# Gate projection in one pass with low weight columns beside the high ones, a 128-row broadcast for the mLSTM, and max scans ahead of the sums

## The chip, the cores and the metric

The program runs on one core of a Trainium2 chip. The metric is the device time of one execution in microseconds; the median of three runs of the kernel before is 877.35 us (877.31 to 877.92). An engine is named as in the profile: PE multiplies matrices (its weight loads are listed apart as PEld), DVE works on vectors, ACT applies functions and copies with a scale, POOL does small general work, and SP starts most transfers.

## The reference

One layer of an encoder over 512 tokens of width 1024. Its first third mixes tokens with two groups of heads, HGRN2 and mLSTM; cross-attention and a squared-ReLU MLP follow. The change touches the gates of the mLSTM group only:

```python
proj = xn @ w_in + b_in          # 16 of its columns are the mLSTM gates
ig_fwd, ig_bwd = ...             # input gates, 4 heads x 2 directions
lfg = log_sigmoid(m_fg)          # forget gates, 4 heads x 2 directions
# per head and direction, over time t and s <= t (or s >= t, backward):
cum   = cumsum(lfg)
log_d = cum[t] - cum[s] + ig[s]
m_t   = max(max_s log_d, cum + m)          # running maximum
d_mat = exp(log_d - m_t)
h_out = (scores * d_mat) @ v / max(|den|, exp(-m_t))
```

## The kernel before, in words

**Products in three passes.** Every large product keeps float32 accuracy by writing each operand as a high and a low part: ACT copies the high part in a rounded format and DVE subtracts it from the source (`split_out`, L222). `mm3` (L226) then issues three matmuls: high by high, high by low, low by high (L227, L228, L229).

**The weight stream.** The weights lie in 512 KB tiles in the order of use (`SEQ`). `weights` (L214) keeps three split tiles, named `wh` and `wl`, and loads a fourth ahead. A tile of the form "d" holds 128 output columns; `proj_d` (L240) makes 8 x 3 = 24 matmuls of 128x128 by 128x512 from it. Below, such a group of 24 is a column. The gate tile is one of these; only 16 of its 128 output columns are used (four each at 0, 32, 64 and 96), the others are zero.

**Chains and ticks.** Work that depends on long rows of small steps is written as generators ("chains"). `proj_d` calls `tick` (L178) after the first 12 matmuls of a column and after the column; a tick runs one chain up to its next `yield`. With several chains in the list, the number of ticks so far, odd or even, says which of the first two runs. `drain` (L191) ticks until no chain is left.

**Order on the engines.** Until L943 a planner places the instructions: on each engine it takes those that its own estimate has ready, in the order of the program, while the split of weights has precedence. So PE mostly follows the program, and small work of DVE, ACT and POOL may be placed early, or a PE step that is not ready be placed some matmuls later. From L943 the order on PE is that of the text.

**The gates.** `gates_proj` (L461) makes the gate rows (`grow`) with 24 matmuls. `gates_chain` (L471) then takes nine ticks while `hgrn_proj(0)` makes six columns: transposes of `grow` (L475) and the logarithm of the sigmoid in `lf` (L477 to L494); sums over time by triangular matmuls (L502); a transpose of `lf` from the tile `lp` into rows `lrow` (L524 to L529); four scans along 512 tokens, for each direction the running maximum `mr` and then the running sum `Fr` (L545, L547); the difference of the two, split into a high and a low half in `ar` (L550 to L552); transposes of `mr` (L556) and their exponential `em` (L558).

**The use of `ar`.** `mlstm_chain` (L594) broadcasts, for each of four heads and two directions, one row of `ar` over all 128 partitions: the column of `selr` that picks the row is the stationary operand, and two matmuls of 64 rows by 512, high and low (L601, L602), add up in PSUM. DVE adds a mask (L605), ACT takes ten exponentials of 128x128 (L612).

Of the kernel before, what the change touches and what calls it, by code (L numbers as in the profile page):

```python
# [18 lines left out]
P = 128  # L19
# [60 lines left out]
def trunk(ctx: ExitStack, tc: tile.TileContext, x, mem, wpk, vec, cst, lmask, rmask, rows, out):  # L80
# [64 lines left out]
    def small_setup():  # L145
        lmf = A4()
        nc.sync.dma_start(out=vc, in_=vec)
        nc.sync.dma_start(out=lmf[:, 0:len(LEVELS) * P], in_=lmask)
        v.tensor_copy(lm, lmf[:, 0:len(LEVELS) * P])
        le, lr = tiny(8), tiny(8)  # L150
        lg = vc[:, V_LB:V_LB + 8]
        v.tensor_tensor(out=le, in0=lg, in1=lg, op=ALU.subtract)
        sc.activation(le, le, AF.Exp)
        v.reciprocal(lr, le)
        v.tensor_tensor(out=le, in0=le, in1=lr, op=ALU.mult)
        v.tensor_tensor(out=lb[:, 0:8], in0=le, in1=le, op=ALU.subtract)
        v.tensor_scalar(out=lb[:, 8:16], in0=lb[:, 0:8], scalar1=-1.0, scalar2=1.0, op0=ALU.mult, op1=ALU.add)
        v.tensor_copy(selr, cs[:, C_SEL:C_SEL + 8])
        v.tensor_scalar(out=negb, in0=vc[:, V_FF:V_FF + 8], scalar1=-1.0, scalar2=None, op0=ALU.mult)

    selr = sb.tile([P, 8], F32R, name="selr")
# [298 lines left out]

    def gates_proj():  # L461
        gh, gl = weights(("d", "gate", 0, 0))
        ps = mmb()
        for k in range(8):
            z = slice(k * P, k * P + P)
            mm3(ps, gh[:, z], gl[:, z], xs[k][0], xs[k][1], k == 0, k == 7)
        grow = A4()
        sc.activation(grow[:, 0:512], ps, AF.Identity, bias=vc[:, V_GATE:V_GATE + 1])
        ml["grow"] = grow

    def gates_chain():  # L471
        grow = ml["grow"]
        ps = smb()
        for t in range(4):
            pe.transpose(ps[:, t * P:t * P + P], grow[:, t * P:t * P + P], ident)  # L475
        gt = sb.tile([P, 64], F32, name="gt")
        v.tensor_copy(gt[:, :].rearrange("p (w g h) -> p w g h", g=4, h=4), ap(ps, 0, [P, 4], [32, 4], [1, 4]))  # L477
        ig = ap(gt, 0, [16, 4], [1, 8])
        z = ap(gt, 8, [16, 4], [1, 8])
        w3 = lambda t: t[:, :].rearrange("p (w c) -> p w c", c=8)  # L480
        az, u, s, s2, pl = tiny(32), tiny(32), tiny(32), tiny(32), tiny(32)
        v.scalar_tensor_tensor(out=w3(az), in0=z, scalar=-1.0, in1=z, op0=ALU.mult, op1=ALU.min)
        sc.activation(u, az, AF.Exp)
        v.tensor_scalar(out=s, in0=u, scalar1=2.0, scalar2=None, op0=ALU.add)
        v.reciprocal(s, s)
        v.tensor_tensor(out=s, in0=s, in1=u, op=ALU.mult)
        v.tensor_tensor(out=s2, in0=s, in1=s, op=ALU.mult)
        v.tensor_scalar(out=pl, in0=s2, scalar1=1.0 / 17, scalar2=1.0 / 15, op0=ALU.mult, op1=ALU.add)
        for n in (13, 11, 9, 7, 5, 3, 1):
            v.tensor_tensor(out=pl, in0=pl, in1=s2, op=ALU.mult)  # L490
            v.tensor_scalar(out=pl, in0=pl, scalar1=1.0 / n, scalar2=None, op0=ALU.add)
        v.scalar_tensor_tensor(out=pl, in0=pl, scalar=-2.0, in1=s, op0=ALU.mult, op1=ALU.mult)
        lf = tiny(32)
        v.scalar_tensor_tensor(out=w3(lf), in0=z, scalar=0.0, in1=w3(pl), op0=ALU.min, op1=ALU.add)  # L494
        for _ in range(4):
            yield

        tri = A4()
        nc.sync.dma_start(out=tri[:, 0:640], in_=cst[:, NC1:NC_])
        pb = smb()  # L500
        for i, c in enumerate((C_INC, C_SUF, C_ISUF, C_PRE, C_ONE)):
            pe.matmul(pb[:, i * 32:i * 32 + 32], lhsT=tri[:, c:c + P], rhs=lf, start=True, stop=True)  # L502
        bd = sb.tile([P, 128], F32, name="bd")
        b4 = lambda g, w, dr: bd[:, g * 32 + w * 8 + dr * 4:g * 32 + w * 8 + dr * 4 + 4]
        bg = lambda g, dr: ap(bd, g * 32 + dr * 4, [8, 4], [1, 4])
        pg = lambda i, dr: ap(pb, i * 32 + dr * 4, [8, 4], [1, 4])
        igd = lambda dr: ap(gt, dr * 4, [16, 4], [1, 4])
        for dr in range(2):
            v.tensor_tensor(out=bg(0, dr), in0=igd(dr), in1=pg(2 * dr, dr), op=ALU.subtract)
            v.tensor_tensor(out=bg(1, dr), in0=igd(dr), in1=pg(2 * dr + 1, dr), op=ALU.add)  # L510
        tot = lambda w, dr: pb[:, 128 + w * 8 + dr * 4:128 + w * 8 + dr * 4 + 4]
        gp.memset(bd[:, 64:128], 0.0)
        for w in (0, 1):
            v.tensor_tensor(out=b4(2, w, 0), in0=b4(1, w, 0), in1=tot(w + 1, 0), op=ALU.add)
            v.tensor_tensor(out=b4(2, 3 - w, 1), in0=b4(1, 3 - w, 1), in1=tot(2 - w, 1), op=ALU.add)
        v.tensor_tensor(out=b4(3, 0, 0), in0=b4(2, 0, 0), in1=tot(2, 0), op=ALU.add)
        v.tensor_tensor(out=b4(3, 3, 1), in0=b4(2, 3, 1), in1=tot(1, 1), op=ALU.add)
        ml["bd"] = lambda g, w, dr, h: bd[:, g * 32 + w * 8 + dr * 4 + h:g * 32 + w * 8 + dr * 4 + h + 1]
        yield

        lp = A4()
        gp.memset(lp[:, 0:512], 0.0)
        for dr in range(2):
            v.tensor_copy(ap(lp, dr * 32, [P, 4], [1, 4]), ap(lf, dr * 4, [8, 4], [1, 4]))  # L524
        ps = smb()
        for t in range(4):
            pe.transpose(ps[:, t * P:t * P + P], lp[:, t * P:t * P + P], ident)
        lrow = grow[:, 512:1024]
        sc.activation(lrow[0:64, 0:512], ps[0:64, :], AF.Copy)  # L529
        rm = lp[:, 512:1024]  # L530
        nc.sync.dma_start(out=rm[0:64, 0:512], in_=rmask)
        yield
        fm = A4()
        Fr, mr = fm[:, 0:512], fm[:, 512:1024]
        gp.memset(Fr[0:64, 0:512], 0.0)
        gp.memset(mr[0:64, 0:512], 0.0)

        def rows_ap(t, dr):
            a = t[0:4, 0:512] if dr == 0 else t[32:36, 0:512]
            if dr == 0:  # L540
                return a
            return bass.AP(a.tensor, a.offset + 511, [list(a.ap[0]), [-1, 512]])

        for dr in range(2):
            v.tensor_tensor_scan(out=rows_ap(mr, dr), data0=rows_ap(lrow, dr), data1=rows_ap(grow, dr),  # L545
                                 initial=0.0, op0=ALU.add, op1=ALU.max)
            v.tensor_tensor_scan(out=rows_ap(Fr, dr), data0=rows_ap(rm, dr), data1=rows_ap(lrow, dr),  # L547
                                 initial=0.0, op0=ALU.mult, op1=ALU.add)
        yield
        v.tensor_tensor(out=Fr[0:64, 0:512], in0=Fr[0:64, 0:512], in1=mr[0:64, 0:512], op=ALU.subtract)  # L550
        ar = big.tile([64, 1024], F32R, name="ar")
        split_out(ar[:, 0:512], ar[:, 512:1024], Fr[0:64, 0:512])  # L552
        ml["ar"] = ar
        ps = smb()
        for t in range(4):
            pe.transpose(ps[:, t * 64:t * 64 + 64], mr[0:64, t * P:t * P + P], ident[0:64, 0:64])  # L556
        em = sb.tile([P, 32], F32, name="em")
        sc.activation(em[:, :].rearrange("p (w g h) -> p w g h", g=2, h=4), ap(ps, 0, [64, 4], [32, 2], [1, 4]), AF.Exp, scale=-1.0)  # L558
        ml["em"] = em
        yield  # L560

    mv = []
# [31 lines left out]
    def mlstm_chain(h, gate):  # L594
# [2 lines left out]
        bcol, ar, em = ml["bd"], ml["ar"], ml["em"]  # L597
        for dr in range(2):
            pa = smb()
            lw = selr[0:64, dr * 4 + h:dr * 4 + h + 1].to_broadcast([64, P])  # L600
            pe.matmul(pa, lhsT=lw, rhs=ar[:, 0:512], start=True, stop=False)  # L601
            pe.matmul(pa, lhsT=lw, rhs=ar[:, 512:1024], start=False, stop=True)  # L602
            am = T2()
            cm = cs[:, C_MF + dr * P:C_MF + dr * P + P]
            v.tensor_tensor(out=am[:, 0:512].rearrange("p (w t) -> p w t", t=P), in0=pa[:, :].rearrange("p (w t) -> p w t", t=P),  # L605
                            in1=cm.unsqueeze(1).to_broadcast([P, 4, P]), op=ALU.add)
            for ws in range(4):
                for wt in (range(ws, 4) if dr == 0 else range(0, ws + 1)):
                    gap = abs(wt - ws)
                    col = ws * 640 + ((wt - ws) * P if dr == 0 else (4 - ws) * P + wt * P)  # L610
                    src = (am if gap == 0 else pa)[:, wt * P:wt * P + P]
                    sc.activation(St[:, col:col + P], src, AF.Exp, bias=bcol(gap, ws, dr, h))  # L612
            yield
# [72 lines left out]
    gates_proj()  # L686
    chains.append(gates_chain())
    hgrn_proj(0)
    drain()
    hgrn_start(0)  # L690
    hgrn_gate(0)
    hgrn_proj(1)
# [430 lines left out]
```

## Time and profile before

| | us |
|---|---|
| median of three runs | 877.35 |
| the profiled execution | 877.47 |
| its span on the chip | 875.7 |
| DVE busy in the span | 576.2 |
| ACT busy in the span | 415.5 |
| POOL busy in the span | 67.4 |

The span runs from the first to the last instruction of the execution; 1.8 us of the profiled execution's time lie around it. A row of the timeline gives the start of an instruction in us from the start of the span, its length, its engine and line, its output and inputs with shapes, and in brackets how long the engine was idle before it and what ended that. The length of a matmul includes the time in which the next one is already running, so the cost of a matmul in a dense stream is the distance between two starts, not its length. A row of the waits gives the total, the number and the longest of the waits of one line for another.

### The profile page before, as it was taken

How to read it: one execution, taken by the hardware profiler on the slowest of the kernel's cores; microseconds unless marked ns; L12 is line 12 of the kernel's file. 1: busy time of each engine (PE TensorE's matmuls, PEld its weight loads, DVE VectorE, ACT ScalarE, POOL GpSimd, SP SyncE). 2: the span in 40 equal slices, each digit the busy share in tenths (PEclk: the TensorE clock that was granted, in tenths of full speed). 3: DMA queues.
4: the chain of work that ended last, by engine and by line, in shares of the span. 5: the costliest groups of instructions: out<-in, count | busy, mean ns of one | idle time of the engine just before them, and what ended most of it. 6: DMA issues, size and time to landing. Idle time of an engine off the chain costs nothing.

```text
span 875.7 us, 11191 instructions
## 1 busy us (share of the span) xinstructions
PE 853.6 (97%) x4198; PEld 709.3 (81%) x4198; DVE 576.2 (66%) x1006; ACT 415.5 (47%) x758; POOL 67.4 (8%) x114
## 2 busy tenths in 40 slices
PE   7999999999999999999999999999999999999995
PEld 5887888888887886888888887888888888888884
DVE  5557688779536987654655445776667656766675
ACT  5235343353358658534544355553355345435544
POOL 2000000010001000000000200002200310121001
PEclk9999999999999999999999999999999999999998
DMA  7322222311234223352212772238945993598322
GB/s 261 135 98 79 73 73 73 117 63 50 73 99 117 97 98 120 121 169 84 85 51 71 194 190 82 92 116 212 284 143 127 238 279 109 150 284 217 115 55 96
DMA packets 32680, 113.58 MB, mean 130 GB/s; under 512 B 3761, under 2 KB 3889, under 8 KB 32626
## 3 DMA queue, kind: packets, MB, share of 16 engines
q1 hardware_dynamic: 23120, 78.84, 26.1%
q0 software_dynamic: 9216, 33.56, 17.2%
q8 instruction: 33, 0.54, 0.2%
q10 hardware_dynamic: 290, 0.47, 0.1%
q14 instruction: 21, 0.17, 0.1%
HBM read 110.76 MB, written 2.10 MB: 129 GB/s over the span
## 4 chain that ended last, share of the span: by engine, by line
PE 49%; DVE 1%; ACT 0%; POOL 0%; issue 0%; POOLq 0%; ACTq 0%
PE mm L228 10%; PE mm L229 10%; PE mm L227 10%; PE sm L997 5%; PE sm L999 5%; PE sm L998 5%; PE mm L999 1%; PE mm L998 1%; PE mm L997 1%; PE sm L229 1%; PE sm L228 1%; PE sm L227 1%; PE sm L770 0%; PE sm L827 0%; DVE vv L922 0%; ACT t L756 0%
## 5 line engine op out<-in xcount | busy, mean ns | idle before, releaser
L223 ACT ACTIVATE wh<-st 128x1024 fp32r<-128x1024 f32 x133 | 140.9, 1059 | 233.1 <-PE mm L228 115.4
L224 DVE TENSOR_TENSOR wl<-st,wh 128x1024 fp32r<-128x1024 f32 x133 | 162.7, 1223 | 124.3 <-ACT wh L223 120.6
L227 PE MATMUL mm<-xT,wh 128*128 128x512 f32 x552 | 219.7, 399 | 0.0
L228 PE MATMUL mm<-xT,wh 128*128 128x512 f32 x552 | 216.4, 392 | 0.2 <-DVE xT L776 0.2
L229 PE MATMUL mm<-xT,wl 128*128 128x512 f32 x552 | 215.8, 391 | 0.0
L228 PEld LDWEIGHTS mm<-xT,wh 128*128 128x128 f32 x552 | 103.8, 188 | 22.7 <-DVE xT L776 2.0
L229 PEld LDWEIGHTS mm<-xT,wl 128*128 128x128 f32 x552 | 103.6, 188 | 21.7 <-issue 0.2
L227 PEld LDWEIGHTS mm<-xT,wh 128*128 128x128 f32 x552 | 103.8, 188 | 21.4 <-issue 1.2
L891 POOL DMA_DIRECT2D as<-in_wpk x48 | 36.6, 772 | 312.1 <-DVE wl L224 188.1
L955 DVE SCALAR_TENSOR_TENSOR t<-mm,rg 128x512 f32<-128x512 f32 x32 | 22.1, 691 | 55.2 <-PE mm L229 55.0
L229 PE MATMUL mm<-wh,yT 128*128 128x512 f32 x128 | 50.6, 395 | 0.0
L227 PE MATMUL mm<-wh,yT 128*128 128x512 f32 x128 | 50.5, 394 | 0.0
L228 PE MATMUL mm<-wl,yT 128*128 128x512 f32 x128 | 50.0, 391 | 0.0
L999 PE MATMUL sm<-wh,yT 128*128 128x512 f32 x128 | 49.8, 389 | 0.0
L998 PE MATMUL sm<-wl,yT 128*128 128x512 f32 x128 | 49.8, 389 | 0.0
L997 PE MATMUL sm<-wh,yT 128*128 128x512 f32 x128 | 49.8, 389 | 0.0
L223 ACT ACTIVATE wh<-as 128x1024 fp32r<-128x1024 f32 x24 | 25.5, 1062 | 33.3 <-PE sm L999 23.7
L224 DVE TENSOR_TENSOR wl<-as,wh 128x1024 fp32r<-128x1024 f32 x24 | 29.4, 1225 | 13.9 <-ACT wh L223 13.9
L378 PEld LDWEIGHTS sm<-a,t 128*128 128x128 f32 x224 | 30.1, 191 | 2.2 <-ACT t L368 0.4
L930 DVE TENSOR_TENSOR vv<-vv,sm 128x512 f32<-128x512 f32 x48 | 31.0, 680 | 1.2 <-PE sm L999 1.2
L368 ACT ACTIVATE t<-a 128x512 f32<-128x512 f32 x28 | 18.4, 674 | 26.3 <-DVE a L431 23.8
L378 PE MATMUL sm<-a,t 128*128 128x128 f32 x224 | 30.9, 285 | 0.0
(258 smaller groups left out, 1513.5 us busy)
## 6 DMA issues: line engine op xcount, KB each, us to landing
st<-in_wpk SPq DMA_DIRECT2D x133, 512.0 KB, 3.3
as<-in_wpk POOLq DMA_DIRECT2D x48, 512.0 KB, 6.7
gate<-in_wpk POOLq DMA_DIRECT2D x16, 512.0 KB, 7.2
as<-in_x SPq DMA_DIRECT2D x4, 512.0 KB, 6.5
vv<-in_x SPq DMA_DIRECT2D x8, 256.0 KB, 4.3
out<-vv SPq DMA_DIRECT2D x7, 256.0 KB, 2.3
a<-in_mem SPq DMA_DIRECT2D x2, 512.0 KB, 3.9
t<-in_rows SPq DMA_DIRECT2D x2, 256.0 KB, 5.9
```

The source lines that it names most:

```text
L223: sc.activation(dst_hi, src, AF.Copy)
L224: v.tensor_tensor(out=dst_lo, in0=src, in1=dst_hi.bitcast(F32), op=ALU.subtract)
L227: pe.matmul(ps, lhsT=ah, rhs=bh, start=first, stop=False)
L228: pe.matmul(ps, lhsT=ah, rhs=bl, start=False, stop=False)
L229: pe.matmul(ps, lhsT=al, rhs=bh, start=False, stop=last)
L378: pe.matmul(ps[:, z], lhsT=kc[:, z], rhs=ap(q2, w * P, [2 * L, P // (2 * L)], [512 + L, 2], [1, L]), start=True, stop=True)
L891: gp.dma_start(out=dst, in_=wpk[idx], **kw)
L930: v.tensor_tensor(out=z, in0=z, in1=ps, op=ALU.add if sign > 0 else ALU.subtract)
L955: v.scalar_tensor_tensor(out=y, in0=ps, scalar=0.0, in1=rrow[:, 0:512], op0=ALU.max, op1=ALU.mult)
L997: pe.matmul(ps, lhsT=ah, rhs=bh, start=new, stop=False, **fl)
L998: pe.matmul(ps, lhsT=ah, rhs=bl, start=False, stop=False, **fl)
L999: pe.matmul(ps, lhsT=al, rhs=bh, start=False, stop=end and k == 1, **fl)
```

## The change

It edits eight places. In `gates_proj` one DVE copy puts the 16 low columns (`gl`) into unused columns of the high tile (`gh`), 16 columns to the right of their high counterparts; two matmuls for each of eight slices remain. The low part's result comes out in rows of its own, and `gates_chain` adds it after the transpose. As the rows of `grow` no longer hold the full sum, the input gates go through the transpose of `lp` too, and a second ACT copy puts them back into rows. The two max scans come ahead of the two sum scans, with a `yield` between; the transposes of `mr` come ahead of the split of `ar`. `ar` now holds the high half in partitions 0 to 63 and the low half in 64 to 127, `selr` is written to both halves of its tile, and the broadcast is one matmul. A `drain()` goes.

```diff
-        v.tensor_copy(selr, cs[:, C_SEL:C_SEL + 8])
+        v.tensor_copy(selr[0:64, :], cs[0:64, C_SEL:C_SEL + 8])
+        v.tensor_copy(selr[64:128, :], cs[0:64, C_SEL:C_SEL + 8])
...
         gh, gl = weights(("d", "gate", 0, 0))
+
+        v.tensor_copy(ap(gh, 16, [P, 8], [32, 4], [1, 4]), ap(gl, 0, [P, 8], [32, 4], [1, 4]))
         ps = mmb()
         for k in range(8):
             z = slice(k * P, k * P + P)
-            mm3(ps, gh[:, z], gl[:, z], xs[k][0], xs[k][1], k == 0, k == 7)
+            pe.matmul(ps, lhsT=gh[:, z], rhs=xs[k][0], start=k == 0, stop=False)
+            pe.matmul(ps, lhsT=gh[:, z], rhs=xs[k][1], start=False, stop=k == 7)
...
-        v.tensor_copy(gt[:, :].rearrange("p (w g h) -> p w g h", g=4, h=4), ap(ps, 0, [P, 4], [32, 4], [1, 4]))
+        g4 = gt[:, :].rearrange("p (w g h) -> p w g h", g=4, h=4)
+        v.tensor_copy(g4, ap(ps, 0, [P, 4], [32, 4], [1, 4]))
+        v.tensor_tensor(out=g4, in0=g4, in1=ap(ps, 16, [P, 4], [32, 4], [1, 4]), op=ALU.add)
...
             v.tensor_copy(ap(lp, dr * 32, [P, 4], [1, 4]), ap(lf, dr * 4, [8, 4], [1, 4]))
+            v.tensor_copy(ap(lp, 64 + dr * 32, [P, 4], [1, 4]), igd(dr))
...
         sc.activation(lrow[0:64, 0:512], ps[0:64, :], AF.Copy)
+        sc.activation(grow[0:64, 0:512], ps[64:128, :], AF.Copy)
...
             v.tensor_tensor_scan(out=rows_ap(mr, dr), data0=rows_ap(lrow, dr), data1=rows_ap(grow, dr),
                                  initial=0.0, op0=ALU.add, op1=ALU.max)
+        yield
+        for dr in range(2):
             v.tensor_tensor_scan(out=rows_ap(Fr, dr), data0=rows_ap(rm, dr), data1=rows_ap(lrow, dr),
                                  initial=0.0, op0=ALU.mult, op1=ALU.add)
         yield
-        v.tensor_tensor(out=Fr[0:64, 0:512], in0=Fr[0:64, 0:512], in1=mr[0:64, 0:512], op=ALU.subtract)
-        ar = big.tile([64, 1024], F32R, name="ar")
-        split_out(ar[:, 0:512], ar[:, 512:1024], Fr[0:64, 0:512])
-        ml["ar"] = ar
         ps = smb()
         for t in range(4):
             pe.transpose(ps[:, t * 64:t * 64 + 64], mr[0:64, t * P:t * P + P], ident[0:64, 0:64])
...
+        v.tensor_tensor(out=Fr[0:64, 0:512], in0=Fr[0:64, 0:512], in1=mr[0:64, 0:512], op=ALU.subtract)
+        ar = big.tile([P, 512], F32R, name="ar")
+        sc.activation(ar[0:64, :], Fr[0:64, 0:512], AF.Copy)
+        v.tensor_tensor(out=ar[64:128, :], in0=Fr[0:64, 0:512], in1=ar[0:64, :].bitcast(F32), op=ALU.subtract)
+        ml["ar"] = ar
         yield
...
-            lw = selr[0:64, dr * 4 + h:dr * 4 + h + 1].to_broadcast([64, P])
-            pe.matmul(pa, lhsT=lw, rhs=ar[:, 0:512], start=True, stop=False)
-            pe.matmul(pa, lhsT=lw, rhs=ar[:, 512:1024], start=False, stop=True)
+            pe.matmul(pa, lhsT=selr[:, dr * 4 + h:dr * 4 + h + 1].to_broadcast([P, P]), rhs=ar, start=True, stop=True)
...
     hgrn_proj(0)
-    drain()
     hgrn_start(0)
```

## The prediction

> **What bounds the kernel now.** I read the page's head first, then the waits of PE, then the busy time by stretches, then the timeline around each edit.
>
> ```profile
> span 875.7 us, 11191 instructions
> PE 853.6 (97%) x4198; PEld 709.3 (81%) x4198; DVE 576.2 (66%) x1006; ACT 415.5 (47%) x758; POOL 67.4 (8%) x114
> ```
>
> PE is busy in 97% of the span, no other engine in more than 66%. Busy can hide waits, so the whole list of what PE's matmuls waited for is next:
>
> ```profile
> PE sm L300 <- DVE as L297: 3.4, 1, 3.4
> PE mm L143 <- DMA rg<-in_rows: 2.3, 1, 2.3
> PE sm L452 <- DVE t L445: 2.1, 3, 0.8
> PE sm L556 <- DVE a L545: 1.7, 1, 1.7
> PE sm L452 <- ACT a L223: 0.6, 1, 0.6
> PE sm L300 <- issue: 0.4, 1, 0.4
> PE sm L725 <- DVE a L716: 0.3, 1, 0.3
> PE mm L228 <- DVE xT L776: 0.2, 1, 0.2
> PE sm L527 <- DVE a L524: 0.2, 1, 0.2
> ```
>
> These nine rows are all. After the start (L143, L300) PE waits some 5 us in the whole span, and no row names the weight tiles `wh` or `wl`: neither transfers nor the split hold PE up. Later it runs without a gap:
>
> ```profile
> 650.00:700.00 50.00, 50.00 (x222) 41.42 (x221) 35.01 (x46) 21.50 (x25) 8.48 (x12) 1.00 0.66 174
> ```
>
> That is a stretch of the MLP: PE busy 50 of 50 us with 222 matmuls, at full granted clock (1.00). So a matmul taken out anywhere, or a wait that goes, moves all that follows to the left, up to the end, unless something else then is late. The sum needs three things: the matmuls that go, the waits that go, and new waits.
>
> **Part 1, gate projection.** Eight of 24 matmuls go (the low weights by the high input).
>
> ```profile
> 37.60 0.39 PE L227 MATMUL mm<-xT,wh 128*128 128x512 f32 x1
> ...
> 43.04 0.39 PE L227 MATMUL mm<-xT,wh 128*128 128x512 f32 x1
> ```
>
> The gate column starts at 37.60, the next one at 43.04: 5.44 us for 24, 0.227 us each. A row's length of 0.39 would be wrong, as the next matmul runs inside it. 8 x 0.227 = **1.81 us** less.
>
> What it adds is a DVE copy of 128x128 numbers, for which the first gate matmul waits. The trace has none of this shape: the split of a tile eight times as wide takes 1.22 us (next rows), two copies of 128x16 take 0.24 (L524, further below). I take 0.25 us. Its cover is idle DVE time:
>
> ```profile
> 28.52 1.22 DVE L224 TENSOR_TENSOR wl<-st,wh 128x1024 fp32r<-128x1024 f32 x1 [1.46 <-ACT wh L223]
> 33.51 1.22 DVE L224 TENSOR_TENSOR wl<-st,wh 128x1024 fp32r<-128x1024 f32 x1 [3.76 <-ACT wh L223]
> ...
> 37.80 0.69 DVE L319 TENSOR_TENSOR vv<-mm,t 128x512 f32<-128x512 f32 x1 [0.67 <-PE mm L229]
> ```
>
> The gate tile is the fifth of the stream. With three tiles held, its split starts when the second is released; counting releases, it is the one at 28.52, done at 29.74. DVE then idles 3.76 us. A planner that places ready work early puts the copy there, 8 us ahead of 37.60, and nothing is paid. If the copy stays at its place in the text, it is queued behind the last L319 (ends 38.49), and the first gate matmul starts near 38.9: 1.3 us. Ends 0 and 1.3; I take 0.
>
> The tile is then released 1.8 us earlier, and the stream moves as a whole.
>
> **Part 2, the gates chain.** The end of its first half, then what PE loses here now:
>
> ```profile
> 53.30 0.18 DVE L494 SCALAR_TENSOR_TENSOR tiny<-gt,tiny 128x32 f32<-128x32 f32 x1
> ...
> 57.14 1.20 PE L502 MATMUL sm<-tiny,a 128*128 128x32 f32 x10
> ```
>
> The addition into `gt`, a small DVE step like L494 (0.18 us), lengthens a chain that is done at 53.48 and is needed by PE at 57.14: 3.66 us of cover, so 0. The second copy of `selr` is small like those of L524, needed only near 270 us; between 0 and 0.2 us if it delays the start, I take 0.
>
> ```profile
> 63.97 0.39 PE L228 MATMUL mm<-xT,wh 128*128 128x512 f32 x1
> 64.52 0.63 PE L527 MATMUL sm<-cs,a 128*128 128x128 f32 x4 [0.17 <-DVE a L524]
> ...
> 67.51 0.39 PE L228 MATMUL mm<-xT,wh 128*128 128x512 f32 x1
> 69.58 0.43 PE L556 MATMUL sm<-cs,a 64*128 64x64 f32 x4 [1.68 <-DVE a L545]
> ```
>
> ```profile
> 64.13 0.24 DVE L524 COPY a<-tiny 128x16 f32<-128x16 f32 x2
> 65.88 1.21 DVE L545 TENSOR_TENSOR_SCAN a<-a 4x512 f32<-4x512 f32 x1 [1.50 <-ACT a L529]
> 67.02 1.19 DVE L547 TENSOR_TENSOR_SCAN a<-a,a 4x512 f32<-4x512 f32 x1
> 68.22 1.21 DVE L545 TENSOR_TENSOR_SCAN a<-a 4x512 f32<-4x512 f32 x1
> ```
>
> ```profile
> 65.19 0.59 ACT L529 ACTIVATE a<-sm 64x512 f32<-64x512 f32 x1 [1.93 <-PE sm L527]
> ```
>
> The transposes of `mr` (L556) stand one tick, 12 matmuls, behind L527. The second max scan, third of four on DVE, ends only at 69.43. From 67.51 to 69.58 are 2.07 us where 0.227 is the rule: **1.84 us** lost. The new text moves both sides. On DVE, two max scans in a row end about 1.2 us earlier (the length of the sum scan between them), but wait for a second ACT copy, 0.59 us like L529: net 0.6 us. On PE, one more `yield` puts L556 a tick later, 12 x 0.227 = 2.72 us. Counted from the start of L527, `mr` was ready for PE after 5.06 us (69.58 - 64.52) and will be after 4.5; PE arrived after 3.22 (67.51 + 0.227 - 64.52) and will arrive after 5.9. The margin is 1.4 us, so the whole 1.84 goes. The tick does most of it; the order of the scans alone would have saved 0.6. What waits for the sums, now last, is `ar`, first used near 270 us.
>
> L527 gets later, as DVE has two more copies ahead of it. It costs 0.32 us now (64.52 - 63.97 - 0.227). L524's two copies take 0.24 us; two more cost another 0.24 if nothing hides them. Their source `gt` is there before L494 reads it at 53.30, so they may be placed early; and the planner may move L527 back a matmul. Ends -0.32 and +0.24; I take **+0.12**, half of what two exposed copies cost.
>
> Taking out `drain()` takes out nothing: the chain had nine ticks, now has ten, and six columns give twelve. It does shift the count of ticks by one, so from here on the second head of each pair goes first. The work is the same; I cost it at 0, the cover being the projections beside it. Its ends: the four L452 waits in the list above, 2.7 us, all go; or all eight heads wait the longest, 0.8 us: 6.4 - 2.7 = 3.7 us more.
>
> **Part 3, the row broadcast.** One of two matmuls goes, for four heads and two directions.
>
> ```profile
> 270.07 0.49 PE L601 MATMUL sm<-ar,selr 64*128 64x512 f32 x1
> 270.40 0.39 PE L602 MATMUL sm<-ar,selr 64*128 64x512 f32 x1
> 270.63 0.39 PE L601 MATMUL sm<-ar,selr 64*128 64x512 f32 x1
> ```
>
> ```profile
> L602 PE MATMUL sm<-ar,selr x8: 385/392/394, 270.4 to 329.7; 64*128 64x512 f32 x8
> ```
>
> From the start at 270.40 to the next are 0.23 us for 64 rows; the 128-row matmuls of Part 1 take 0.227, so the wider pass costs no more than one narrow one. 8 x 0.23 = **1.84 us**. Ends: 0, if PE then waits for the exponentials behind it, and 2.6 us, at the 0.33 that a first pass takes after another kind of matmul (270.07 to 270.40).
>
> [...]
>
> **The sum.** 1.81 + 1.84 + 1.84 - 0.12 = 5.37 us. From the profiled execution, 877.47 us (span 875.7 and 1.8 around it, both unchanged in kind), that is **872.1 us**; the median of the runs shown, 877.35, lies 0.12 lower, which I neglect.
>
> **The rivals.**
>
> *The wait at L556 stays.* DVE puts a split of weights (1.22 us) and the work on a finished column between the two max scans: more than the 1.4 us of margin. For it: a split comes with every column, some 5.4 us, and the two max scans take 2.4. Against: the rows above show three scans in a row, with no split between. If all 1.84 us stay: 874.0.
>
> *The copy into the gate tile is late*, behind the last L319: 1.3 us, 873.4. Against it: 3.76 us of idle DVE time lie right ahead of it.
>
> *A pass taken out is worth less than the distance of two starts*, because half of that distance is something else that stays. The lowest price that the trace bears out is that of matmuls half as wide:
>
> ```profile
> 319.54 0.28 PE L228 MATMUL mm<-a,wh 128*128 128x256 f32 x1
> 319.66 0.28 PE L229 MATMUL mm<-a,wl 128*128 128x256 f32 x1
> ```
>
> 16 x 0.12 = 1.9 us in place of 3.65: 873.8. Against it: 222 matmuls in 50 us of the MLP, mostly of 512 columns and without a wait, leave no room inside 0.227. [...]
>
> *The swapped heads take it back.* All eight wait at L452 as above: 872.1 + 3.7 = 875.8, no change that can be measured.
>
> *Slower: the swapped order uncovers the exponentials.* In the mLSTM stretch PE needs ten exponentials per head and direction before a product.
>
> ```profile
> L612 ACT ACTIVATE as<-sm,bd x48: 348/364/404, 272.6 to 346.1; 128x128 f32<-128x128 f32 x48
> L612 ACT ACTIVATE as<-t,bd x32: 388/402/443, 272.3 to 346.4; 128x128 f32<-128x128 f32 x32
> ```
>
> (48 x 0.364 + 32 x 0.402) / 8 = 3.8 us for a group. If the projections beside them no longer cover two groups, PE waits 7.6 us: 872.1 + 7.6 = 879.7. One group gives 875.9; from two on the kernel is slower. For it: with the second matmul of the broadcast gone PE has a little less to do between the mask and the product. Against: the list of PE's matmul waits has no row for L616 or L631, and the two heads of a pair do equal work.
>
> **How the numbers follow.** A measurement of this kernel tells about 0.2%, 1.75 us, from no change. Chances: forecast 0.63; wait at L556 stays 0.12; late copy 0.08; cheaper passes 0.02; swapped heads take it back 0.10; slower 0.05. The first four are faster by more than 0.2% (under 875.6): 0.85; within: 0.10; slower: 0.05. Likeliest: 872.1. Range 870.2 to 875.2: below, L527 hidden and half of the L452 waits gone (0.5 + 1.4 us); above, wait and late copy together (1.84 + 1.3). The two last cases, 0.15, are left out.
>
> **What would show it.** PE x4182 on the page. The next column 3.63 us after the start of the gate column, and a DVE copy in the idle time ahead of it. No row L556 among PE's waits; L527 under 0.4 us. One 128x512 matmul at the line of the broadcast, eight times, followed after 0.23 to 0.33 us. L452 waits of 2 to 4 us. It would be wrong if PE waited for ACT or DVE where the list above has no row, above all between 250 and 370 us, or if column starts there did not come some 5 us earlier.

## The result and the profile after

The changed kernel takes 872.05 us (median of 4 runs, 871.84 to 872.46) against 877.63 us for the kernel before in the same session (4 runs, 877.31 to 878.52): a ratio of 0.9935, interval 0.9923 to 0.9947. The profiled execution after took 872.23 us. The forecast was 872.1, range 870.2 to 875.2.

Where PE keeps its wait of 1.7 us near 68 us, the times of a kernel fall into two groups 1.4 to 2.0 us apart, and in some executions the granted clock falls to 0.50 behind that wait; of the 53 executions of the kernel before that were run beside all kernels here, 36 lie at 876.92 to 877.75, 15 at 878.21 to 879.55, and two between.

The head of the page of the kernel after (span, then busy time, share and instructions by engine):

```profile
span 870.5 us, 11166 instructions
...
PE 848.8 (98%) x4182; PEld 707.3 (81%) x4182; DVE 577.4 (66%) x1011; ACT 416.1 (48%) x759; POOL 67.6 (8%) x114
```

16 matmuls are gone, PE is busy for 4.8 us less, and the span is 5.2 us shorter. What PE waited for in the kernel after (total us, times, longest):

```profile
PE sm L301 <- DVE as L298: 3.0, 1, 3.0
PE sm L453 <- DVE t L446: 2.9, 4, 1.1
PE mm L143 <- DMA rg<-in_rows: 2.4, 1, 2.4
PE mm L228 <- DVE tiny L647: 1.6, 1, 1.6
PE mm L229 <- DVE xT L784: 0.3, 1, 0.3
PE sm L733 <- DVE a L724: 0.3, 1, 0.3
PE sm L640 <- DVE as L630: 0.2, 1, 0.2
```

Lines have moved: the old L527 is L534, L556 is L562, L452 is L453, and `mm3` has L228 to L230. The transposes of `mr` and of `lp` have left the list. A new row has come in: a matmul of a weight column (L228) waits 1.6 us for DVE.

Where the 5.2 us came from is read off the starts of matmuls that stand at the same place of the work. From the timeline of the kernel before (start, length): the sixth column after the gate column, the first column of the second pair of mLSTM projections, the second column of the output projection, and the last matmul of all.

```profile
75.06 0.39 PE L227 MATMUL mm<-xT,wh 128*128 128x512 f32 x1
...
259.17 0.47 PE L227 MATMUL mm<-xT,wh 128*128 128x512 f32 x1
...
376.74 0.39 PE L227 MATMUL mm<-wh,yT 128*128 128x512 f32 x1
...
864.38 0.39 PE L999 MATMUL sm<-wh,a 128*128 128x512 f32 x1
```

The same places in the kernel after, with the gate column and the column behind it ahead of them:

```profile
37.83 0.39 PE L469 MATMUL mm<-xT,wh 128*128 128x512 f32 x1
...
41.45 0.39 PE L228 MATMUL mm<-xT,wh 128*128 128x512 f32 x1
...
71.70 0.39 PE L228 MATMUL mm<-xT,wh 128*128 128x512 f32 x1
...
255.83 0.47 PE L228 MATMUL mm<-xT,wh 128*128 128x512 f32 x1
...
371.51 0.39 PE L228 MATMUL mm<-wh,yT 128*128 128x512 f32 x1
...
859.15 0.39 PE L1007 MATMUL sm<-wh,a 128*128 128x512 f32 x1
```

| stretch | before, us | after, us | gain | forecast |
|---|---|---|---|---|
| start to the gate column | 37.60 | 37.83 | -0.23 | 0 |
| the gate column | 5.44 | 3.62 | 1.82 | 1.81 |
| to the sixth column after it (scans) | 32.02 | 30.25 | 1.77 | 1.84 - 0.12 |
| to the second mLSTM projections | 184.11 | 184.13 | -0.02 | 0 |
| to the output projection (broadcast) | 117.57 | 115.68 | 1.89 | 1.84 |
| to the last matmul | 487.64 | 487.64 | 0.00 | 0 |

Each row is the difference of two starts above, or of 37.60 and 43.04 from the prediction. The first row is not the change's: other kernels below, with and without its parts, reach the gate column between 36.9 and 37.9 us.

The three gains stand where they were foretold. Two of them came about in another way than the prediction says, as the experiments show.

### The profile page after: what moved, and what is told of

It reads as the page before. It is cut to its first block, busy times and chain, and to the rows that moved or that the text cites. A ratio compares the mean times of both kernels' runs of the same rounds, so it can differ in the third digit from the quotient of the medians.

```text
span 870.5 us, 11166 instructions
## 1 busy us (share of the span) xinstructions
PE 848.8 (98%) x4182; PEld 707.3 (81%) x4182; DVE 577.4 (66%) x1011; ACT 416.1 (48%) x759; POOL 67.6 (8%) x114
## 4 chain that ended last, share of the span: by engine, by line
PE 50%; DVE 1%; ACT 0%; POOL 0%; issue 0%; POOLq 0%; ACTq 0%
PE mm L229 10%; PE mm L230 10%; PE mm L228 10%; PE sm L1005 5%; PE sm L1006 5%; PE sm L1007 5%; PE mm L1006 1%; PE mm L1005 1%; PE mm L1007 1%; PE sm L230 1%; PE sm L229 1%; PE sm L228 1%; PE sm L778 0%; PE sm L835 0%; DVE vv L930 0%; ACT t L764 0%
## 5 line engine op out<-in xcount | busy, mean ns | idle before, releaser
L225 DVE TENSOR_TENSOR wl<-st,wh 128x1024 fp32r<-128x1024 f32 x133 | 162.9, 1225 | 119.5 <-ACT wh L224 115.9
L228 PE MATMUL mm<-xT,wh 128*128 128x512 f32 x544 | 215.7, 397 | 0.0
L229 PE MATMUL mm<-xT,wh 128*128 128x512 f32 x544 | 213.2, 392 | 0.3 <-DVE xT L784 0.3
L230 PE MATMUL mm<-xT,wl 128*128 128x512 f32 x544 | 213.3, 392 | 0.0
L229 PEld LDWEIGHTS mm<-xT,wh 128*128 128x128 f32 x544 | 102.3, 188 | 21.8 <-DVE xT L784 2.0
L230 PEld LDWEIGHTS mm<-xT,wl 128*128 128x128 f32 x544 | 102.2, 188 | 21.8 <-issue 0.7
L228 PEld LDWEIGHTS mm<-xT,wh 128*128 128x128 f32 x544 | 102.3, 188 | 20.6 <-issue 0.5
L230 PE MATMUL mm<-wh,yT 128*128 128x512 f32 x128 | 50.6, 395 | 0.0
L228 PE MATMUL mm<-wh,yT 128*128 128x512 f32 x128 | 50.4, 394 | 0.0
L225 DVE TENSOR_TENSOR wl<-as,wh 128x1024 fp32r<-128x1024 f32 x24 | 29.4, 1226 | 14.2 <-ACT wh L224 14.2
```

The source lines that it names most:

```text
L225: v.tensor_tensor(out=dst_lo, in0=src, in1=dst_hi.bitcast(F32), op=ALU.subtract)
L228: pe.matmul(ps, lhsT=ah, rhs=bh, start=first, stop=False)
L229: pe.matmul(ps, lhsT=ah, rhs=bl, start=False, stop=False)
L230: pe.matmul(ps, lhsT=al, rhs=bh, start=False, stop=last)
```

## The experiments

**One part at a time.** The first four kernels ran beside the same 25 executions of the kernel before (median 877.32).

*The gate projection alone.* Into the kernel before go the copy into `gh`, the two-matmul loop, the addition into `gt`, and what keeps the rows right (the input gates through `lp`, the second ACT copy).

```diff
+        v.tensor_copy(ap(gh, 16, [P, 8], [32, 4], [1, 4]), ap(gl, 0, [P, 8], [32, 4], [1, 4]))
-            mm3(ps, gh[:, z], gl[:, z], xs[k][0], xs[k][1], k == 0, k == 7)
+            pe.matmul(ps, lhsT=gh[:, z], rhs=xs[k][0], start=k == 0, stop=False)
+            pe.matmul(ps, lhsT=gh[:, z], rhs=xs[k][1], start=False, stop=k == 7)
...
+        sc.activation(grow[0:64, 0:512], ps[64:128, :], AF.Copy)
```

> The gate projection alone, with the input gates sent through the transpose and the second ACT copy; scans, tick of the transposes of mr, split of ar, broadcast and drain as before. Theory (the terms add up): the next column starts 1.81 us earlier after the gate column, and the transposes of mr still wait, since PE comes a tick too early: 1.8 us or up to 0.6 more for the second copy. Time 1.2 to 1.8 us under before. Rival (the second copy costs nothing because DVE runs a sum scan while it waits): the wait stays at 1.8 and all of 1.81 arrives. Rival (a matmul taken out is worth 0.12 us): 1 us or less.

Measured: 876.14 us (10 runs), ratio 0.9986, interval 0.9977 to 0.9995. But the ten lie in two groups: five at 874.84 to 875.68 and five at 876.60 to 877.40. The profiled run is of the second. In its trace the gate column is 1.81 us shorter, as foretold, and the wait at the transposes of `mr` (here L562) is as before. What differs is the granted clock right behind that wait. Busy time by stretches; the column after POOL's is the granted clock of PE:

```profile
PE sm L562 <- DVE a L551: 1.7, 1, 1.7
```

```profile
68.50:69.00 0.50, 0.50 (x3) 0.37 (x2) 0.50 (x1) 0.50 (x1) 0.00 (x0) 0.71 0.00 0
69.30:70.90 1.60, 1.60 (x5) 1.22 (x5) 1.60 (x3) 0.20 (x1) 0.00 (x0) 0.50 0.00 0
```

A mean of 0.71 over the first of the two stretches is full clock up to 68.71 and half clock from there. At half clock the matmuls start 0.43 us apart in place of 0.227; the half clock lasts 3.41 us, to 72.12 (a mean of 0.88 from 72.00 to 72.50), and eight such distances cost 1.6 us by estimate (8 x 0.20). The wait itself did not grow for the second ACT copy, as the first rival has it: here too one sum scan goes first on DVE (64.48), ahead of the max scans (65.62). Against the lower group of before (about 877.2) the lower group here, about 875.3, is 1.9 less: the term of 1.81 holds.

*The broadcast alone.* `selr` in both halves, `ar` as 128 rows, one matmul.

```diff
-            pe.matmul(pa, lhsT=lw, rhs=ar[:, 0:512], start=True, stop=False)
-            pe.matmul(pa, lhsT=lw, rhs=ar[:, 512:1024], start=False, stop=True)
+            pe.matmul(pa, lhsT=selr[:, dr * 4 + h:dr * 4 + h + 1].to_broadcast([P, P]), rhs=ar, start=True, stop=True)
```

> The 128-row broadcast alone: selr in both halves, ar in two halves of partitions, one matmul for two; the rest as before, head order too. Theory: 8 matmuls at 0.23 us, 1.84 us under before, spread over the stretch from 255 to 370 us, where the changed kernel gained 1.85 net. Rival (the changed kernel's new wait of 1.6 us near 305 us, on DVE, comes from the swapped heads): no such wait here, and the gain in that stretch is 2.5 us or more. Rival (PE now runs ahead of DVE there): the wait is here too and the net gain stays below 2 us.

Measured: 876.27 us (10 runs), ratio 0.9985, interval 0.9976 to 0.9994; five at 875.34 to 875.76 and five at 876.79 to 878.20. From its waits of PE, the old wait and a new one:

```profile
PE sm L558 <- DVE a L546: 1.7, 1, 1.7
PE mm L228 <- DVE tiny L638: 1.6, 1, 1.6
```

The half clock comes later here: the clock is full from the end of the wait (69.36) to 70.90, then 0.53 on average over 3.4 us.

```profile
70.90:74.30 3.40, 3.40 (x11) 2.58 (x10) 3.37 (x6) 2.11 (x3) 0.00 (x0) 0.53 0.33 100
```

What follows: between the same two places of the work as in the table (the second mLSTM projections and the output projection) the broadcast brings 1.57 us net, and it alone brings the new wait of a weight column, as the second rival has it. The heads are not swapped in this kernel, so the swap is not its cause.

*The tick alone.* One more `yield` behind the scans, all else as before: max, sum, max, sum on DVE, and the heads swapped by the extra tick.

```diff
                                  initial=0.0, op0=ALU.mult, op1=ALU.add)
         yield
+        yield
```

> The kernel before with one more yield ahead of the step that transposes mr; scan order, gate, broadcast as before. The count of ticks shifts by one, so the heads of each pair swap. Theory: the tick alone takes out the whole wait at the transposes of mr, 1.84 us, and the swapped heads cost nothing between 80 and 370 us (under 0.3 us). Rival (the order of the scans is needed): part of the wait stays. Rival (the swap costs): a loss of about 1.6 us between 255 and 370 us, and the time is within 0.3 us of before.

Measured: 875.49 us (10 runs, 875.08 to 875.86, one group), ratio 0.9975, interval 0.9966 to 0.9984. The two groups of transposes in its timeline:

```profile
64.24 0.63 PE L527 MATMUL sm<-cs,a 128*128 128x128 f32 x4 [0.17 <-DVE a L524]
...
69.82 0.46 PE L557 MATMUL sm<-cs,a 64*128 64x64 f32 x4
```

No bracket stands behind L557: PE comes 5.6 us after L527, and `mr` is ready. The whole wait is gone by the tick alone, and the upper group of times with it. The gain stays constant from 91 to 543 us, so swapped heads cost nothing.

*The heads put back.* The changed kernel with the count of ticks set back by one.

```diff
     hgrn_proj(0)
+    turn[0] -= 1
     hgrn_start(0)
```

> The changed kernel with the count of ticks set back by one where the drain was, so that the first head of each pair goes first as before. Theory (swap is neutral): the time of the changed kernel, 872.0 plus or minus 0.4 us, and the wait of a kv matmul on DVE near 305 us is still there. Rival (the swap made that wait): it is gone, and the time is 870.4.

Measured: 871.72 us (4 runs), ratio 0.9936, interval 0.9919 to 0.9952; the starts of its columns, less the start-up, agree with the changed kernel's to 0.02 us, and the new wait of 1.6 is there. The order of the heads plays no part.

**The tick or the order of the scans?** The next four ran beside 15 executions of before (median 877.41). The first takes the second `yield` out of the changed kernel and keeps its order of scans.

```diff
                                  initial=0.0, op0=ALU.add, op1=ALU.max)
-        yield
         for dr in range(2):
```

> The changed kernel without its second yield: the transposes of mr stand one tick (12 matmuls) behind those of lp, as before, while the gate column, the broadcast and the order of the scans in the text are the changed ones. Theory (the tick took the wait away, the order of the scans took nothing, since one sum scan still runs first on VectorE): in the trace of the changed kernel the second max scan ends 4.9 us after the start of the transposes of lp, and TensorE comes after about 3.2, so the wait is back with about 1.7 us and the time is 871.9 + 1.7 = 873.6; in the executions where the granted clock halves behind the wait another 1.6, 875.2, so two groups of times. Rival (the order of the scans counts, the yield does not): wait under 0.5 us, time 872.0 to 872.4, one group.

Measured: two runs at 873.18 and 873.77, three at 875.08 to 875.26; median 875.08, ratio 0.9960, interval 0.9947 to 0.9972. Its timeline and its stretch behind the wait:

```profile
67.88 0.43 PE L561 MATMUL sm<-cs,a 64*128 64x64 f32 x4 [1.66 <-DVE a L553]
```

```profile
68.20:71.70 3.50, 3.50 (x10) 2.71 (x9) 3.47 (x6) 1.11 (x3) 0.00 (x0) 0.53 0.16 34
```

The wait is back in full, and the profile of this kernel, too, shows the half clock behind it. So in the changed kernel the order of the scans saves nothing and the tick everything. Why is seen in the changed kernel's own rows, of DVE and then of ACT:

```profile
64.42 1.21 DVE L557 TENSOR_TENSOR_SCAN a<-a,a 4x512 f32<-4x512 f32 x1 [1.49 <-issue]
65.56 2.41 DVE L553 TENSOR_TENSOR_SCAN a<-a 4x512 f32<-4x512 f32 x2
```

```profile
63.74 0.59 ACT L536 ACTIVATE a<-sm 64x512 f32<-64x512 f32 x1 [2.08 <-PE sm L534]
64.36 0.60 ACT L537 ACTIVATE a<-sm 64x512 f32<-64x512 f32 x1
```

L557 is a sum scan (the other one follows at 67.91), L553 the max scans. A sum needs only the first ACT copy (L536); a max needs the second as well (L537, done at 64.96). The planner therefore issued one sum scan first, and the max scans end at 67.97, no earlier against the transposes of `lp` than before.

*The order alone, without the second copy*: the kernel before with the scans in two loops.

```diff
             v.tensor_tensor_scan(out=rows_ap(mr, dr), data0=rows_ap(lrow, dr), data1=rows_ap(grow, dr),
                                  initial=0.0, op0=ALU.add, op1=ALU.max)
+        for dr in range(2):
             v.tensor_tensor_scan(out=rows_ap(Fr, dr), data0=rows_ap(rm, dr), data1=rows_ap(lrow, dr),
```

> The kernel before with one edit: both max scans ahead of both sum scans, no yield, no second copy by ScalarE, old gate column and broadcast. Theory: max scans really come first on VectorE here, since grow needs no copy; the second one ends 2.4 us after the first starts instead of 3.6. The transposes of mr stand 11 matmuls behind those of lp in the order of issue, two earlier than before, so TensorE comes after 2.8 us and mr is ready after 3.8: wait 1.0 us, 0.8 less than before, 876.3. If the halved clock needs a wait of about 1.7 us, the upper group of times (878 and above) is gone and the times lie within 0.5 us of each other. Rival 1 (any wait sets it off): still two groups 1 to 2 us apart. Rival 2 (the wait is not set by the second max scan): 877.1, nothing gained.

Measured: 876.51 us (11 runs, 876.02 to 877.37), ratio 0.9987, interval 0.9978 to 0.9996. From its timeline, DVE, then PE, and the stretch behind the wait:

```profile
65.27 2.44 DVE L545 TENSOR_TENSOR_SCAN a<-a 4x512 f32<-4x512 f32 x2 [1.51 <-ACT a L529]
```

```profile
67.85 0.43 PE L557 MATMUL sm<-cs,a 64*128 64x64 f32 x4 [1.00 <-DVE a L545]
```

```profile
67.90:71.30 3.40, 3.40 (x17) 2.79 (x18) 3.35 (x4) 1.34 (x3) 0.00 (x0) 1.00 0.00 0
```

Here the max scans do come first, the wait falls from 1.7 to 1.0 us, and the clock behind it stays full. No run lies at 878 or above, but the spread is 1.35 us and not the 0.5 that was expected; one profile does not settle whether a wait of 1.0 us never sets off the half clock.

*A longer wait*: the kernel before with the second max scan done four times over, same output.

```diff
-            v.tensor_tensor_scan(out=rows_ap(mr, dr), data0=rows_ap(lrow, dr), data1=rows_ap(grow, dr),
-                                 initial=0.0, op0=ALU.add, op1=ALU.max)
+            for _ in range(4 if dr == 1 else 1):
+                v.tensor_tensor_scan(out=rows_ap(mr, dr), data0=rows_ap(lrow, dr), data1=rows_ap(grow, dr),
+                                     initial=0.0, op0=ALU.add, op1=ALU.max)
```

> The kernel before with the second max scan (dr 1) done four times over, with the same output: three scans of 1.2 us more on VectorE ahead of the transposes of mr, which the order of issue puts 26 matmuls behind the transposes of lp instead of 12 to 13. Reckoned from the trace of before, TensorE comes at about 6.3 us after the start of the transposes of lp and mr is ready after about 11: a wait of 4 to 5 us in place of 1.8. Theory (a wait of TensorE is followed by half the granted clock for about 3.4 us, the surer the longer the wait): half clock behind the wait in the profile, 1.6 us, and no two groups of times any more; 877.1 + 2.2 to 3.2 + 1.6 = 880.9 to 881.9. Rival (the half clock has nothing to do with the wait, it is chance): full clock in most executions, 879.3 to 880.3 with a tail above.

Measured: 882.01 us (5 runs, 881.61 to 883.26), ratio 1.0048, interval 1.0036 to 1.0061. The wait, and the clock behind it:

```profile
75.82 0.66 PE L557 MATMUL sm<-cs,a 64*128 64x64 f32 x4 [4.38 <-DVE a L546]
```

```profile
75.80:79.10 3.30, 3.28 (x10) 2.64 (x11) 1.59 (x3) 0.78 (x2) 0.00 (x0) 0.50 0.01 2
```

All five runs are in the range of the theory (880.9 to 881.9) or above it, none in that of chance (879.3 to 880.3). Two columns on, the start is 4.3 us later, start-up aside, than in the kernel before: 2.7 for the longer wait and 1.6 for the half clock.

**The new wait.** In the changed kernel, the timeline of DVE and then of PE around it:

```profile
304.13 1.23 DVE L225 TENSOR_TENSOR wl<-st,wh 128x1024 fp32r<-128x1024 f32 x1 [0.24 <-ACT wh L224]
305.27 0.68 DVE L602 SCALAR_TENSOR_TENSOR yT<-t,t 128x512 f32<-128x512 f32 x1
...
305.95 0.41 DVE L225 TENSOR_TENSOR a<-mm,a 128x256 fp32r<-128x256 f32 x1
```

```profile
303.83 1.06 PE L640 MATMUL sm<-vv,as 128*128 128x129 f32 x8
306.51 0.35 PE L228 MATMUL mm<-a,wh 128*128 128x256 f32 x1 [1.62 <-DVE tiny L647]
```

PE is through with eight products at 304.9 and wants the next column of `kv`, the fifth. There are four result buffers, so the first `kv` column must be split out of its buffer by DVE before (L225, `a<-mm`); that column was finished at 288.60, but its split stands in DVE's order behind other work, at the end a weight split and a convolution step, and ends at 306.36, just before PE goes on. The row names L647, which ran in between; the buffer is the likelier cause, and the next kernel tests it: the changed kernel with a high priority for these splits.

```diff
-            split_out(kT[i][:, j * 512:j * 512 + 256], kT[i][:, j * 512 + 256:j * 512 + 512], ps[:, :256])
+            with tc.high_priority():
+                split_out(kT[i][:, j * 512:j * 512 + 256], kT[i][:, j * 512 + 256:j * 512 + 512], ps[:, :256])
```

> The changed kernel with one edit: the splits of the kv columns (VectorE's second half of each, out of the TensorE result) get a high priority, so VectorE's order of issue has them ahead of the convolution steps that stood in front of them. Theory: the new wait of 1.6 us near 305 us is TensorE waiting for a result buffer that such a split releases late; with the split ahead the wait goes and the time falls by 1.4 to 1.6, to 870.3 to 870.5. Rival 1: the buffer is only handed to the next late operation (convolution or mask product), the wait moves to another row and the time stays at 871.9. Rival 2: the convolution steps that are put back delay the mLSTM products, TensorE waits there, 873 or more.

Measured: 871.10 us (5 runs, 870.62 to 871.55), ratio 0.9922, interval 0.9910 to 0.9934. Its waits of PE between 255 and 375 us are the L733 row as in the changed kernel, and this one:

```profile
PE sm L453 <- DVE t L446: 3.8, 3, 1.6
```

The wait of the column is gone, so the theory had its cause right. But the heads' transposes (L453) now wait 3.8 us here, where the changed kernel has 2.5, and only 0.64 us of the 1.6 are left as gain at the output projection. A part of the wait moved on, which was the first rival, and its size lies between the two.

*More room for the heads.* With the kv splits ahead, and without, a second `yield` between the scaling of a head and its transposes; the changed kernel again beside them. These three ran beside 9 executions of before (median 877.64).

```diff
                         in1=r.unsqueeze(2).to_broadcast([P, 4, P]), op=ALU.mult)
         yield
+        yield
```

> The changed kernel with the kv splits ahead and a second yield in the finish of each head, between the scaling of the head and its transposes. Theory: a tick more lets VectorE's scaling end before TensorE comes, as it did for the transposes of mr; the four waits of the head transposes, 4.2 us in the trace with the kv splits ahead, shrink to under 1, and the time falls from 871.1 by 2.5 to 3.5 to 867.6 to 868.6. Rival 1: the heads end one tick later each, and where the columns run out before the chains do, the transposes are issued with no projection beside them: 871 or more. Rival 2: VectorE stays late in this stretch, the wait moves to the products of the next head or to a result buffer: 870 to 871.

> The changed kernel with the second yield in the finish of each head alone, the kv splits where the change has them. Theory: the four waits of the head transposes (2.9 us) go, the wait of the kv column near 305 us (1.6 us) stays: 871.9 - 2.5 = 869.4. Rival 1 (ticks run out): 871.9 or more. Rival 2 (the wait of the kv column is fed by the same late VectorE queue and goes or grows with the heads' order): 868 or 871.

> The changed kernel itself, on the same chip as the two versions above. All theories: 871.7 to 872.5, in one narrow group, as the transposes of mr do not wait any more.

Measured, five runs each: 871.19 us (ratio 0.9925, interval 0.9912 to 0.9937) with both edits, 871.62 us (0.9929, 0.9917 to 0.9942) with the `yield` alone, 871.66 us (0.9932, 0.9919 to 0.9946) for the changed kernel (871.60 to 872.38, where 871.7 to 872.5 was expected). Neither theory of the second `yield` held; whether the ticks ran out, as the first rival of each has it, is not shown. PE's waits between 255 and 375 us with the `yield` alone:

```profile
PE sm L454 <- DVE t L446: 2.7, 3, 1.0
PE sm L454 <- DVE tiny L649: 1.1, 1, 1.1
```

That is 3.8 us; the wait of the `kv` column, which was to stay with the `yield` alone, is not among them. With both edits the list sums to 3.6 (1.9, 1.1 and 0.6), against 4.6 in the changed kernel and 4.1 with the kv splits ahead. Four orders of the same work move PE's waits from row to row and leave 3.6 to 4.6 us of them; before, it was 2.6 (1.7, 0.6 and 0.3). DVE is behind most of these rows. Work that stands at 285 to 300 us in the kernel after stands 3.34 us later in the kernel before (255.83 and 259.17 us above). Busy time of that work, the columns being PE, PEld, DVE, ACT and POOL, of the kernel before and of the kernel after:

```profile
288.50:303.50 15.00, 15.00 (x101) 12.96 (x100) 14.94 (x25) 9.43 (x19) 0.13 (x2) 1.00 0.32 106
```

```profile
285.00:300.00 15.00, 15.00 (x109) 13.32 (x108) 14.96 (x25) 10.68 (x21) 0.13 (x2) 1.00 0.35 115
```

In the whole span DVE is at 66%; in this stretch it is full in both kernels, 14.94 and 14.96 of 15 us. (The same stretch of the clock, 285 to 300 us, has 13.66 in the kernel before, but that is other work.) So DVE did not become full by the change: before, it was full too, and PE came just late enough. The split that frees the first `kv` buffer and the start of the fifth `kv` column, in the kernel before:

```profile
308.63 0.41 DVE L224 TENSOR_TENSOR a<-mm,a 128x256 fp32r<-128x256 f32 x1
...
309.60 0.28 PE L227 MATMUL mm<-a,wh 128*128 128x256 f32 x1
```

The buffer is free at 309.04 and PE needs it at 309.60, a margin of 0.56 us. In the kernel after, with the 3.34 us added, PE is there at 308.2, 1.4 us earlier, and the split ends at 309.7, 0.7 us later. That the L453 waits, too, come from DVE's load is argued from these rows and from the waits that only move; no kernel with less work for DVE was run. Of all versions the one with the kv splits ahead has the lowest median, by 0.1 us (both edits) to 0.9 us; the intervals overlap.

## Why the prediction was right, point by point

*Gate projection, 1.81.* Measured 1.82; the next column starts 3.62 us after the gate column's, 3.63 foretold. The copy was costed at 0 for lying in DVE's idle time behind the fifth split, and there it is (DVE of the kernel after):

```profile
28.74 1.23 DVE L225 TENSOR_TENSOR wl<-st,wh 128x1024 fp32r<-128x1024 f32 x1 [1.46 <-ACT wh L224]
30.07 0.23 DVE L465 CAST wh<-wl 128x128 fp32r<-128x128 f32 x1
```

It takes 0.23 us (0.25 assumed), and DVE then stays idle for 3.43 us. The rival of the late copy falls. So does that of the cheaper passes: the eight were worth 1.82 us. At the 0.12 us of that rival they would have been worth 1.0 us.

*The wait at L556, 1.84.* It is gone, and "the tick does most of it" is right; it does all of it. The step that failed is "on DVE, two max scans in a row end about 1.2 us earlier", and with it the 0.6 us for the order of the scans and the margin of 1.4 us. I took the order of the text for the order on DVE, and did not ask which scan has its inputs first, though I had priced the second ACT copy that only the max scans wait for. The true margin is read from PE of the kernel after:

```profile
62.59 0.39 PE L230 MATMUL mm<-xT,wl 128*128 128x512 f32 x1
63.08 0.63 PE L534 MATMUL sm<-cs,a 128*128 128x128 f32 x4
...
68.12 0.39 PE L230 MATMUL mm<-xT,wl 128*128 128x512 f32 x1
68.44 0.46 PE L562 MATMUL sm<-cs,a 64*128 64x64 f32 x4
```

`mr` is ready 67.97 - 63.08 = 4.9 us after the start of the transposes of `lp`, not 4.5, and PE is there after 68.35 - 63.08 = 5.3, not 5.9, as only 21 matmuls of columns stand between the two groups of transposes, not 24: a margin of 0.4 us. The rival that the wait stays was nearer than its chance of 0.12 says. With the wait the upper group of times went too (15 of 53 executions before, none of four after); the prediction has no term for that.

*The transposes of `lp`, +0.12.* Measured 62.59 to 63.08 less 0.227, that is 0.26 us, where 0.32 were lost before: a gain of 0.06, not a loss. The two more copies were not hidden by being early: on DVE all four run one behind the other, from 62.53 to 62.93, 0.40 us in place of 0.24. But the transposes stand one matmul later than before, behind a third matmul of a triple and not a second (L228 at 63.97), which the prediction names as its other end.

*The broadcast, 1.84.* The net, 1.89, is right, the working is not, and that the two agree is luck. The sum of the distances from the matmul before to each broadcast matmul is 4.33 us for sixteen and 1.69 for eight: 2.64 gross, at the upper bound of 2.6. The prediction priced every pass at 0.23 us, the distance of two passes of 64 rows in the middle of a group. In the kernel before, the sixteen stand in four groups; in each the second starts 0.33 to 0.34 us behind the first, and the next matmul of 128 rows 0.32 us behind the last. Of the new passes of 128 rows, six have the next matmul 0.23 to 0.24 us behind them when that is one of a column; from PE of the kernel after:

```profile
267.09 0.40 PE L611 MATMUL sm<-ar,selr 128*128 128x512 f32 x1
267.33 0.39 PE L229 MATMUL mm<-xT,wh 128*128 128x512 f32 x1
```

Fewer groups are not the reason, as the eight stand in six. That it is the number of rows is likely but not shown: two distances of 0.32 us are left around the new passes, both close behind transposes. Of the 2.64 us, PE's waits in this stretch took 2.0 (4.6 in place of 2.6, the new wait 1.62 of them); the other 1.2 us of gain lie in distances between other matmuls whose order changed, and stay unexplained.

The step that failed here is the new wait put at nothing: the prediction priced only a wait for the exponentials behind the broadcast, and what came is a wait for a result buffer that DVE frees late. Its own sign of being wrong, a wait of PE for DVE between 250 and 370 us in a row not on the list, did show; the two terms that the sum had too small, the cheaper passes and the changed order, happened to make good for it.

*`drain` and the heads, 0.* Right: swapped or not, 871.72 and 871.66 to 872.05 cannot be told apart. The L453 waits went from 2.7 to 2.9 us.

*The exponentials.* No row of PE's waits names them; the rival that ends slower falls.

## What to carry to other kernels

When the busiest engine loses work, look in that very stretch, not in the whole span, for the engine that comes next, and compare two kernels at the same place of the work, not at the same time: here DVE was full there before and after, a result buffer came free 0.56 us ahead of its use, and a good part of what a cheaper pass set free was lost in waits that the reorderings tried did not remove. Where an operation must come first, put the distance on the consumer's side (one tick cost nothing and took the whole wait), since the planner here let whatever had its inputs first go ahead. A wait of 1.7 us of the matrix engine cost its length and, in some executions, 1.6 us more in clock, so such a wait ahead of dense work deserves more than its length in a sum.

## What the runs showed of the hardware

After a PE wait of 1.66 to 1.68 us near 68 us the granted clock was 0.50 for 3.41 us in three of four profiled kernels that had this wait (the gate alone, the broadcast alone, the changed kernel without the tick) and 1.00 in the fourth (the kernel before); it began some 0.5 us behind the end of the wait in two and 1.8 us behind it in one, and, counted from the end of the wait to the start of the 25th matmul of columns behind it, cost 1.60 us without the tick and 1.63 us with the broadcast alone, against the kernel before. After a wait of 1.00 us (the order alone) the clock stayed at 1.00; after one of 4.38 us (the longer wait) it was 0.50 at once, again for 3.41 us.

When the clock falls can be read from the same traces. One more fall to 0.50 lies behind the last matmul of the program; of the gate alone and of the kernel before, by its mean clock:

```profile
867.00:867.50 0.50, 0.00 (x0) 0.00 (x0) 0.50 (x2) 0.02 (x1) 0.00 (x0) 0.93 0.00 0
```

```profile
867.00:867.50 0.50, 0.00 (x0) 0.00 (x0) 0.50 (x2) 0.06 (x1) 0.00 (x0) 0.59 0.00 0
```

That is 867.43 and 867.09 us. In the kernel before the last matmul ends at 864.77, so PE had been idle for 2.32 us at the fall; in the changed kernel, from 859.54 to 861.90, for 2.36 us. With the longer wait the clock stayed at 1.00 through 4.38 us of idle PE and fell at 75.83, as the wait ended; with the gate alone it fell at 68.71, when PE had been at work again for 0.53 us. So the moment of the fall does not follow from the length of the idle time in these traces. Nor does the idle time alone decide whether there is one: behind the wait of 1.68 us in the kernel before the clock stayed full, and so it did, at 1.00 from 300 to 312 us, behind the wait of 1.6 us near 305 us in all five profiles that have it (the broadcast alone, the heads put back, no tick, and two of the changed kernel). What else counts is not shown.

That the upper group of times of the kernel before is the same thing is an inference: no profile of it fell in that group. But the three profiled executions with the half clock are of the upper group of their kernel and the one with full clock is of the lower, and the groups are there where the wait is and gone where it is gone (875.08 to 875.86 with the tick alone).
